# Block products with one destination share a PSUM buffer, the weight sums are spread over the products, and the tail gets a PSUM pool of its own

## The chip, the cores and the metric

The kernel runs on one core of one Trainium2 chip. The metric is the device time of one execution in microseconds. The time before is the median of three runs. Beside it there is one execution that was profiled: a record of every instruction, of every DMA and of the clock that TensorE was granted. The engines are called as in the profile: PE is TensorE's matmul, PEld its weight load, DVE is VectorE, ACT is ScalarE, POOL is GpSimd and SP is SyncE, which here only issues DMAs.

## The reference

One decoder layer on 1024 prompt rows and 8 times 8 sample rows, so 1088 rows in all, of 1024 channels. Only its end matters here: the gated FFN of width 2816, the residual and the last norm.

```
x = x + concatenate([a, o]) @ w_out
h = rms_norm(x, norm_ffn_g)
g = depthwise_conv_valid(concatenate([past, h @ w_ffn_gate]), w, b)
x = x + (silu(g) * (h @ w_ffn_up)) @ w_ffn_down      # the last FFN product
y = rms_norm(x, norm_final_g)
```

All of it is in fp32. `w_ffn_down` is 2816 x 1024.

## The kernel before

**Numbers in two parts.** An fp32 operand is split into hi (a rounded copy, made by ACT) and lo (raw minus hi, made by DVE or POOL). A product of two operands is three matmuls, hi*hi, lo*hi and hi*lo, added up in PSUM.

**The last FFN product by Strassen's scheme.** Its left operand, `w_down`, is cut into 2 x 2 blocks (a11, a12, a21, a22), and so is its right operand, the gated activations. The 22 tiles of 128 along the FFN width make two halves of 11. Of each half 5 tiles form group 0 (`STRASSEN[0]`), 4 tiles group 1, and the last 2 (`PLAIN`) are multiplied plainly in the tail. The scheme is Winograd's form: seven block products for each group in place of eight. The seven right operands, sums of activation blocks among them, were stored to DRAM in `ub` by an earlier stage (UB11, UT1, UB21, UB22, UT3, UT2, UT4). The left operands are a12, a22, a11 as they are, and then four sums of weight blocks, which `weight_sums` makes on DVE, in place.

**One block product** is done for four row tiles m of 128 output channels. For each m, `stationary` makes hi (ACT, L1362) and lo (POOL, L1363) of 128 x n*128 weights (n is 5 or 4), in a ring `AS` of 4 tiles. Then `pair()` takes a PSUM buffer of two banks, and `block_product` issues n tiles x 3 matmuls x 2 halves of 272 columns into it (L911, L913, L914): 30 matmuls in group 0, 24 in group 1. Then DVE adds the buffer to each destination (L1439), a quarter of `x2`: `x2[4*r+m]` is the residual of row block r, h is its left or right half of 544 columns. The destinations are the third member of `PRODUCTS`: 1, 1, 4, 2, 2, 3 and 1 of them. So each of the fourteen products has its own buffers, and every destination is one DVE add from PSUM: 14 adds a group and m, 112 in all.

**Order.** The program runs the products in the order a12, a22, a11, a21, a22, a11, a12. `weight_sums(g, m)`, four DVE operations (L1368 to L1371), stands in the third product, right after the block product of each m. All loads go through `load` (L1325) on SP's queue, each told to issue after the one before. Their order is that of the program: a12, moving operand 0, the left halves of `x2[0..3]`, a22, moving operand 1, two stores of the stage before, the left halves of `x2[4..7]`, a11, moving operand 2, a21, moving operand 3, the right halves of `x2`, and so on. `load_moving` brings n tiles of 128 x 544 into one of three rings of 5 (X1, X0, XA by turns), so the tiles of product q + 3 wait until product q has been multiplied. ACT makes their hi (L1347) and DVE their lo (L1348). Group 1's a12 and a22 are loaded during the fourth and fifth product of group 0, its a11 and a21 at its own first product.

**PSUM.** The pool of this stage has 3 buffers of two banks and 2 single banks (`r`) for the norm. Outside what the code says by `issue_after`, a planner orders the instructions of each engine by a model of their times.

**The tail** (`last_product`) multiplies the last 2 + 2 tiles in four column chunks (`TAIL`: 320, 256, 256, 256). For each chunk and each of eight row tiles it issues 12 matmuls (L1458 to L1460), adds the result to `x2` (L1470) and sums squares (L1472, L1476). Row tiles 2i and 2i + 1 share one buffer of two banks (`tail_bank`). During the next chunk the norm of the one before is finished (`root`, `spread`, L205, L232) and its rows are scaled (L1487) and stored (L1489).

## Time and profile before

| what | us |
|---|---|
| time, median of 3 runs | 1374.52 (1371.86 to 1377.04) |
| the profiled execution's own time | 1372.98 |
| its span, first to last instruction | 1371.2 |
| PE busy in the span | 1319.3 (96%) |
| DVE busy in the span | 965.4 (70%) |
| ACT, POOL busy in the span | 557.7 (41%), 479.0 (35%) |
| stage of the block products, first matmul to last add | 1096.3 to 1303.3 and the add that starts there |
| tail | from there to 1371.2 |

The page cuts the span into 40 slices of 34 us; the two stages above are slices 32 to 39. A busy PE says only that matmuls were in its pipe, so the number of matmuls in a stretch and the granted clock say more than the share. `x504` is a count of instructions. An answer with windows gives for each stretch the busy time and count of each engine, the granted clock, the mean share of the 16 DMA engines and the GB/s. In a list of groups, what stands behind the bar is the busy time, the mean duration of one in ns, and the idle time of the engine just before them with what ended it.

### The profile page before, as it was taken

The page shows a single profiled execution, that of the slowest core. Times are in us where ns is not written, and L with a number is a line of the kernel's source. Part 1 is how long each engine was busy: PE and PEld are TensorE (multiplying, and loading weights), DVE is VectorE, ACT ScalarE, POOL GpSimd, SP SyncE. Part 2 cuts the span into 40 slices and gives each one's busy share as a digit, 9 for nine tenths or more (in the row PEclk, how much of TensorE's full clock was granted, in tenths as well). Part 3 has the DMA queues.
Part 4 walks back from the last instruction along what each step waited for, and adds up shares of the span by engine and source line. Part 5 has one row for each costly group of instructions (what it writes and reads, how often), then busy time and mean ns, then how long its engine had stood idle before and what let it go on. Part 6 is the DMA issues. An engine that isn't in the chain of part 4 may idle for free.

```text
span 1371.2 us, 25956 instructions
## 1 busy us (share of the span) xinstructions
PE 1319.3 (96%) x10275; PEld 1249.3 (91%) x10275; DVE 965.4 (70%) x1825; ACT 557.7 (41%) x1128; POOL 479.0 (35%) x375
## 2 busy tenths in 40 slices
PE   7999999999999999999999999999999997998996
PEld 7998988898978886888999999999999997998995
DVE  6378879456676556778986767767676579679656
ACT  6312211356575556255533333333233443343432
POOL 1221112111111001630665645656545444445600
PEclk9999999999999999999999999999999999999998
DMA  8147684945689777461033323133232492342412
GB/s 283 55 134 272 229 289 163 233 125 139 182 268 282 222 249 232 137 222 56 3 117 119 119 89 120 47 104 119 98 110 82 153 359 100 126 148 89 129 40 93
DMA packets 92762, 210.28 MB, mean 153 GB/s; under 512 B 13792, under 2 KB 42720, under 8 KB 92640
## 3 DMA queue, kind: packets, MB, share of 16 engines
q1 hardware_dynamic: 92640, 208.62, 46.8%
q8 instruction: 81, 1.33, 0.4%
q14 instruction: 41, 0.34, 0.1%
HBM read 152.55 MB, written 56.04 MB: 152 GB/s over the span
## 4 chain that ended last, share of the span: by engine, by line
PE 76%; DVE 12%; DMA 6%; issue 3%; ACT 1%; SPq 1%; POOL 1%; DVEq 0%; ACTq 0%
PE g L185 6%; PE g L183 6%; PE g L184 6%; PE py L913 4%; PE py L911 4%; PE py L914 4%; PE o L735 3%; PE g L911 3%; PE g L913 3%; PE g L914 3%; PE pz L911 3%; PE s L650 3%; PE pz L913 3%; PE pz L914 3%; PE px L911 3%
## 5 line engine op out<-in xcount | busy, mean ns | idle before, releaser
L159 POOL TENSOR_TENSOR wl<-wr,wh 128x1024 fp32r<-128x1024 f32 (+1 forms) x36 | 67.5, 1877 | 343.8 <-PE g L185 263.4
L183 PE MATMUL g<-xh,wh 128*128 128x384 f32 (+1 forms) x472 | 157.9, 335 | 1.9 <-DVE qkv L450 1.2
L911 PE MATMUL g<-ux,as 128*128 128x272 f32 x504 | 147.0, 292 | 12.5 <-DVE x L1439 7.0
L184 PE MATMUL g<-xl,wh 128*128 128x384 f32 (+1 forms) x472 | 156.7, 332 | 0.0
L185 PE MATMUL g<-xh,wl 128*128 128x384 f32 (+1 forms) x472 | 156.7, 332 | 0.0
L914 PE MATMUL g<-ux,as 128*128 128x272 f32 x504 | 146.5, 291 | 0.0
L913 PE MATMUL g<-ux,as 128*128 128x272 f32 x504 | 146.1, 290 | 0.0
L1016 POOL TENSOR_TENSOR wb<-wr,wb 128x512 fp32r<-128x512 f32 x84 | 120.8, 1448 | 57.4 <-ACT wb L1015 57.4
L1363 POOL TENSOR_TENSOR as<-ar,as 128x640 fp32r<-128x640 f32 (+1 forms) x56 | 94.6, 1696 | 108.1 <-ACT as L1362 94.2
L1015 ACT ACTIVATE wb<-wr 128x512 fp32r<-128x512 f32 x84 | 52.4, 628 | 154.4 <-DVE wr L1032 94.6
L1016 POOL TENSOR_TENSOR wa<-wr,wa 128x512 fp32r<-128x512 f32 x42 | 65.9, 1571 | 134.9 <-ACT wa L1015 115.3
L911 PEld LDWEIGHTS g<-ux,as 128*128 128x128 f32 x504 | 96.4, 191 | 14.2 <-ACT ux L1347 6.4
L691 ACT ACTIVATE y<-y,m 128x128 f32<-128x128 f32 (+1 forms) x192 | 88.4, 463 | 20.3 <-DVE m L679 20.2
L914 PEld LDWEIGHTS g<-ux,as 128*128 128x128 f32 x504 | 96.2, 191 | 0.0
L913 PEld LDWEIGHTS g<-ux,as 128*128 128x128 f32 x504 | 96.1, 191 | 0.0
L654 DVE CUSTOM_DVE_ANT_0 y<-s,pmk 128x128 f32<-128x128 f32 (+1 forms) x192 | 64.1, 379 | 44.1 <-PE s L650 34.2
L183 PEld LDWEIGHTS g<-xh,wh 128*128 128x128 f32 x472 | 89.1, 189 | 5.0 <-issue 3.1
L1238 DVE SCALAR_TENSOR_TENSOR fc<-gb,prm,fc 128x1104 f32<-128x1104 f32 x44 | 82.4, 1891 | 14.9 <-ACT fc L1236 14.4
L1439 DVE TENSOR_TENSOR x<-g,x 128x544 f32<-128x544 f32 x112 | 75.0, 715 | 23.7 <-PE g L914 23.6
L185 PEld LDWEIGHTS g<-xh,wl 128*128 128x128 f32 x472 | 89.0, 189 | 2.3 <-issue 2.1
L184 PEld LDWEIGHTS g<-xl,wh 128*128 128x128 f32 x472 | 89.3, 189 | 0.5 <-issue 0.2
L396 DVE SCALAR_TENSOR_TENSOR cacc<-gp,prm,cacc 128x1024 f32<-128x1024 f32 x60 | 84.9, 1415 | 0.0
(370 smaller groups left out, 4259.8 us busy)
## 6 DMA issues: line engine op xcount, KB each, us to landing
cr<-in_kc SPq DMA_DIRECT2D x24, 768.0 KB, 6.4
cr<-in_vc SPq DMA_DIRECT2D x24, 768.0 KB, 7.6
ux<-ub SPq DMA_DIRECT2D x63, 272.0 KB, 4.3
kk<-dk SPq DMA_DIRECT2D x48, 256.0 KB, 6.0
wr<-in_w_gate SPq DMA_DIRECT2D x22, 512.0 KB, 3.3
wr<-in_w_up SPq DMA_DIRECT2D x22, 512.0 KB, 4.3
wr<-in_w_in SPq DMA_DIRECT2D x20, 512.0 KB, 5.4
ub<-u SPq DMA_DIRECT2D x18, 544.0 KB, 4.5
```

Source lines behind the costliest of these rows:

```text
L183: nc.tensor.matmul(ps[c], whi[:, k, :], xh[:, t0:t0 + n], start=(k == 0), stop=False)
L184: nc.tensor.matmul(ps[c], whi[:, k, :], xl[:, t0:t0 + n], start=False, stop=False)
L185: nc.tensor.matmul(ps[c], wlo[:, k, :], xh[:, t0:t0 + n], start=False, stop=(k == nk - 1))
L396: eng.scalar_tensor_tensor(acc[:, :S], gp[:, j:j + S], col(w0 + j), acc[:, :S], op0=ALU.mult, op1=ALU.add)
L691: nc.scalar.activation(y, y, AF.Exp, bias=m[:, 4 * g + i:4 * g + i + 1], scale=-1.0, accum_out=den[:, g, 2 * hd + u, i:i + 1])
L911: nc.tensor.matmul(ps, whi[:, k, :], xh[:, t], start=(start and k == 0), stop=False, skip_group_check=True)
L913: nc.tensor.matmul(ps, whi[:, k, :], xl[:, t], start=False, stop=False, skip_group_check=True)
L914: nc.tensor.matmul(ps, wlo[:, k, :], xh[:, t], start=False, stop=(k == nk - 1), skip_group_check=True)
L1016: nc.gpsimd.tensor_sub(lo, x, hi.bitcast(F32))
L1238: nc.vector.scalar_tensor_tensor(c[:, :W], gb[i][:, t:t + W], col(C_FW + 3 * f + t), c[:, :W], op0=ALU.mult, op1=ALU.add)
L1363: nc.gpsimd.tensor_sub(lo, raw, hi.bitcast(F32))
L1439: nc.vector.tensor_add(x, all_of(ps), x)
```

## The change

The seven products of a group are named P1 to P7 and run in units. A unit of two products runs the first for all four m, then the second for the same four m, and the second adds onto the first's PSUM buffer (`block_product(..., i == 0)` sets no start for it). The buffer is read by DVE after each product: after the first for those destinations that need the first alone, after the second for those that need both.

* Group 0: P2 | P4 | P7 | P1, P6 | P5, P3. Group 1: P2 | P7, P4 | P1, P6 | P5, P3. The adds per m are 1 + 1 + 2 + 1 + 3 + 1 + 1 = 10 in group 0 and 1 + 1 + 1 + 1 + 3 + 1 + 1 = 9 in group 1: 76 in all.
* The weight sums are the same four operations, in three places. `first_sums` (two of them) comes with group 0's P4 (for m of 2 and 3 it may go ahead of their adds) and with group 1's P2; `second_sum` with P1; `last_sum` with P5. The sum s1 takes a22's place in group 0 and gets tiles of its own in group 1.
* Loads: a11, `x2[4..5]`'s left halves and a21 now stand ahead of the two stores and of moving operand 2; then the left halves of `x2[6..7]` and the right halves. Of group 1, a11 is loaded in the unit P1, P6 of group 0, and a21, a22, a12 in its unit P5, P3, behind the moving operands of group 1's first two products. The tail's weights are loaded in the last unit, four row tiles ahead of the activations and four behind.
* PSUM: 4 buffers of two banks for the block products. When these are done the pool is closed and another opened with 6 single banks and 2 for the norm; each row tile of the tail has a bank of its own.

The number of matmuls is the same.

```diff
--- before.py
+++ after.py
@@ -1293,54 +1293,59 @@
         zf.__exit__(None, None, None)
 
 
-        zd = zones("D")
-        zd.__enter__()
-        rbank[0] = ("D", "r", 2)
-        pairs[:] = ["D", 3]
+        side = dict(side="left", reuse_waits="tile")
+        zd, zb, zt_ = [tc.tile_pool(name=s + "D", bufs=1, **kw) for s, kw in (
+            ("sb", side), ("ps", dict(space=PSUM, **side)), ("pt", dict(space=PSUM, **side)))]
+        zone["D"], zone["Dps"] = zd.__enter__(), zb.__enter__()
+        pairs[:] = ["D", 4]
 
         def wide(s, dt=F32):
             return zt("D", "SQ", SQS, s, max(n for _, n in TAIL), dt)
 
         n0 = STRASSEN[0][1]
-        OUT = ("X1", "X0", "XA")
-        RAW = {"a12": "RA", "a22": "RB", "a11": "RC", "a21": "RC"}, {"a12": "RC", "a22": "RC", "a11": "RB", "a21": "RC"}
+        OUT = ("XA", "X0", "X1")
         RAWS = {"RA": 4, "RB": 4, "RC": 12}
+        RAW = ({"a12": "RA", "a22": "RB", "a11": "RC", "a21": "RC"},
+               {"a12": "RB", "a22": "RC", "a11": "RC", "a21": "RC", "s1": "RA"})
         wide("sq")
-        for tag in OUT:
+        for tag in OUT[::-1]:
             zt("D", tag, RING, "uh", N)
         zt("D", "AS", 4, "as", 2 * n0 * P, F32R)
         for tag in ("RC", "RB", "RA"):
             zt("D", tag, RAWS[tag], "ar", n0 * P)
 
-        PRODUCTS = ((UB21, "a12", ((0, 0),)), (UT4, "a22", ((1, 0),)), (UB11, "a11", ((0, 0), (0, 1), (1, 0), (1, 1))),
-                    (UT3, "a21", ((1, 0), (1, 1))), (UT1, "a22", ((0, 1), (1, 1))),
-                    (UT2, "a11", ((0, 1), (1, 0), (1, 1))), (UB22, "a12", ((0, 1),)))
-        jobs = [(g, i) for g in range(len(STRASSEN)) for i in range(len(PRODUCTS))]
-        ring = 0
-        raws, moving, lows = {}, {}, []
+        P1, P2, P3 = (UB11, "a11", ((0, 0),)), (UB21, "a12", ((0, 0),)), (UB22, "a12", ((0, 1),))
+        P4, P5 = (UT4, "a22", ((1, 0),)), (UT1, "s1", ((1, 1),))
+        P6, P7 = (UT2, "a11", ((0, 1), (1, 0), (1, 1))), (UT3, "a21", ((1, 1),))
+        UNITS = [(0, u) for u in ((P2,), (P4,), (P7,), (P1, P6), (P5, P3))]
+        UNITS += [(1, u) for u in ((P2,), (P7, P4), (P1, P6), (P5, P3))]
+        PRODUCTS = [(g, product) for g, unit in UNITS for product in unit]
+        raws, moving, lows, done = {}, [], [], []
         loaded_last = [None]
 
         def load(dst, src):
             with tc.issue_after(loaded_last[0]) if loaded_last[0] else nullcontext():
                 loaded_last[0] = nc.sync.dma_start(dst, src).ins
 
-        def load_raw(g, key):
+        def raw_tiles(g, key):
+            tag = RAW[g][key]
+            raws[g, key] = [zt("D", tag, RAWS[tag], "ar", n0 * P)[:, :STRASSEN[g][1] * P] for _ in range(4)]
+            return raws[g, key]
+
+        def load_raw(g, *keys):
 
             j0, n = STRASSEN[g]
-            h, i = int(key[1]) - 1, int(key[2]) - 1
-            raws[g, key] = []
-            for m in range(4):
-                t = zt("D", RAW[g][key], RAWS[RAW[g][key]], "ar", n0 * P)[:, :n * P]
-                load(t, w_down[4 * h + m][:, (i * HF + j0) * P:(i * HF + j0 + n) * P])
-                raws[g, key].append(t)
+            for key in keys:
+                h, i = int(key[1]) - 1, int(key[2]) - 1
+                for m, t in enumerate(raw_tiles(g, key)):
+                    load(t, w_down[4 * h + m][:, (i * HF + j0) * P:(i * HF + j0 + n) * P])
 
         def load_moving(q):
-            g, i = jobs[q]
+            g, (b, _, _) = PRODUCTS[q]
             j0, n = STRASSEN[g]
-            b = PRODUCTS[i][0]
-            moving[q] = []
+            moving.append([])
             for j in range(j0, j0 + n):
-                t = zt("D", OUT[::-1][q % 3], RING, "ux", N, F32R)
+                t = zt("D", OUT[q % 3], RING, "ux", N, F32R)
                 hi, lo = t[:, :HN], t[:, HN:N]
                 raw = lo.bitcast(F32)
                 load(raw, ub[j][:, b * HN:b * HN + HN])
@@ -1363,14 +1368,23 @@
             nc.gpsimd.tensor_sub(lo, raw, hi.bitcast(F32))
             return [t.rearrange("p (k c) -> p k c", c=P) for t in (hi, lo)]
 
-        def weight_sums(g, m):
-            a11, a12, a21, a22 = [raws[g, k][m] for k in ("a11", "a12", "a21", "a22")]
-            nc.vector.tensor_add(a22, a21, a22)
+        def first_sums(g, m):
+            a11, a21, a22, s1 = [raws[g, key][m] for key in ("a11", "a21", "a22", "s1")]
+            nc.vector.tensor_add(s1, a21, a22)
             nc.vector.tensor_sub(a21, a11, a21)
-            nc.vector.tensor_sub(a11, a22, a11)
+
+        def second_sum(g, m):
+            a11, s1 = raws[g, "a11"][m], raws[g, "s1"][m]
+            nc.vector.tensor_sub(a11, s1, a11)
+
+        def last_sum(g, m):
+            a11, a12 = raws[g, "a11"][m], raws[g, "a12"][m]
             nc.vector.tensor_sub(a12, a12, a11)
 
         w, act = [], []
+
+        def tiles_of(j0, n):
+            return [j for i in range(2) for j in range(j0 + i * HF, j0 + i * HF + n)]
 
         def load_last(k0, k1):
 
@@ -1381,7 +1395,7 @@
                 for i in range(step):
                     load(raw[:, i * 2 * n * P:(i + 1) * 2 * n * P].rearrange("p (i c) -> p i c", i=2),
                          w_down[m0 + i].rearrange("p (i c) -> p i c", i=2)[:, :, j0 * P:(j0 + n) * P])
-                tag = ("RA", "RC", "RC", "RB")[m0 // 2]
+                tag = ("RC", "RC", "RC", "RA")[m0 // 2]
                 for i in range(step):
                     r = raw[:, i * 2 * n * P:(i + 1) * 2 * n * P]
                     hi, lo = [zt("D", tag, RAWS[tag], s, n0 * P, F32R)[:, :2 * n * P] for s in ("wh", "wl")]
@@ -1389,8 +1403,8 @@
                     nc.gpsimd.tensor_sub(lo, r, hi.bitcast(F32))
                     w.append([t.rearrange("p (k c) -> p k c", c=P) for t in (hi, lo)])
 
-        def load_act(j, q):
-            hi, lo = [zt("D", OUT[::-1][q % 3], RING, s, N, F32R) for s in ("ah", "al")]
+        def load_act(j, tag):
+            hi, lo = [zt("D", tag, RING, s, N, F32R) for s in ("ah", "al")]
             raw = lo.bitcast(F32)
             load(raw, ud[j])
             nc.scalar.activation(hi, raw, AF.Copy)
@@ -1404,54 +1418,67 @@
             behind(l, lows[4])
         load_raw(0, "a22")
         load_moving(1)
+        load_raw(0, "a11")
+        reload((4, 5), 0)
+        load_raw(0, "a21")
         for st in stores:
             load(*st)
-        reload(range(4, KT), 0)
-        for q, (g, i) in enumerate(jobs):
-            b, key, outs = PRODUCTS[i]
-            more = g + 1 < len(STRASSEN)
-            if i == 0:
-                load_raw(g, "a11")
-            if q + 2 < len(jobs):
-                load_moving(q + 2)
-            if i == 0:
-                load_raw(g, "a21")
-            if q == 1:
-                reload(range(KT), 1)
-            if i == 3 and more:
-                load_raw(g + 1, "a12")
-            if i == 4 and more:
-                load_raw(g + 1, "a22")
-            if not more:
-                if i in (3, 4, 5, 6):
-                    load_last(2 * (i - 3), 2 * (i - 3) + 2)
-                if i in (5, 6):
-                    for j in range(2):
-                        load_act(PLAIN[0] + j + (i - 5) * HF, len(jobs) + i - 5)
-            for m in range(4):
-                a = stationary(g, key, m)
-                ps = pair()
-                block_product(ps, a, moving[q], True)
-                if i == 2:
-                    weight_sums(g, m)
-                for r, h in outs:
-                    x = x2[4 * r + m][:, h * HN:h * HN + HN]
-                    nc.vector.tensor_add(x, all_of(ps), x)
+        load_moving(2)
+        reload((6, 7), 0)
+        reload(range(4, KT), 1)
+        raws[0, "s1"] = raws[0, "a22"]
+        for k, (g, unit) in enumerate(UNITS):
+            for q in range(len(moving), min(len(done) + len(unit) + 2, len(PRODUCTS))):
+                load_moving(q)
+            if k == 1:
+                reload(range(4), 1)
+            elif k == 3:
+                load_raw(1, "a11")
+            elif k == 4:
+                load_raw(1, "a21", "a22", "a12")
+            elif k == 5:
+                raw_tiles(1, "s1")
+            elif k == 8:
+                load_last(0, 4)
+                for j in tiles_of(*PLAIN):
+                    load_act(j, OUT[2 if j < HF else 0])
+                load_last(4, KT)
+            chain = {}
+            for i, product in enumerate(unit):
+                b, key, outs = product
+                for m in range(4):
+                    a = stationary(g, key, m)
+                    if i == 0:
+                        chain[m] = pair()
+                    block_product(chain[m], a, moving[len(done) + i], i == 0)
+                    if unit == (P7,):
+                        outs = ((1, 0), (1, 1))
+                    for r, h in outs:
+                        x = x2[4 * r + m][:, h * HN:h * HN + HN]
+                        added = nc.vector.tensor_add(x, all_of(chain[m]), x).ins
+                    if g and product is P2:
+                        first_sums(g, m)
+                    elif unit[0] is P4:
+                        if m < 2:
+                            half_done = added
+                        with tc.issue_after(half_done):
+                            first_sums(g, m)
+                    elif product is P1:
+                        second_sum(g, m)
+                    elif product is P5:
+                        last_sum(g, m)
+            done.extend(unit)
+        zb.__exit__(None, None, None)
+        zone["Dps"] = zt_.__enter__()
+        gbank[0], rbank[0] = ("D", "g", 6), ("D", "r", 2)
 
         nj = len(act)
-        held = [None]
-
-        def tail_bank(m):
-            if m % 2 == 0:
-                held[0] = pair()
-            return held[0][:, m % 2 * 512:m % 2 * 512 + 512]
-
 
         def last_product(t0, n, hook):
 
             acc = None
             for m in range(KT):
-                ps = tail_bank(m)
+                ps = bank(*gbank[0])
                 whi, wlo = w[m]
                 with tc.issue_after(summed[0]) if m in (2, 4) and i else nullcontext():
                     for k, (xh, xl) in enumerate(act):
@@ -1509,6 +1536,7 @@
 
             acc = last_product(t0, n, norm_of_last)
         scaled(rstd(acc, D, wide, n)[:, :n], *TAIL[-1])
+        zt_.__exit__(None, None, None)
         zd.__exit__(None, None, None)
         zr.__exit__(None, None, None)
 
```

## The prediction, made before the change was run

> **What bounds the kernel now.** First the page: which engine, and where it isn't full.
>
> ```profile
> PE 1319.3 (96%) x10275; PEld 1249.3 (91%) x10275; DVE 965.4 (70%) x1825; ACT 557.7 (41%) x1128; POOL 479.0 (35%) x375
> PE   7999999999999999999999999999999997998996
> ```
>
> PE bounds the whole. The change touches slices 32 to 39, and of these the second and the fifth show less than a full PE (the 7 and the 8 behind the long run of 9s). Next the list of groups cut to that stage: what PE waited for, and what DVE did there.
>
> ```profile
> L911 PE MATMUL g<-ux,as 128*128 128x272 f32 x504 | 147.0, 292 | 12.5 <-DVE x L1439 7.0 <-ACT ux L1347 4.8 <-ACT as L1362 0.8
> L1439 DVE TENSOR_TENSOR x<-g,x 128x544 f32<-128x544 f32 x111 | 74.3, 715 | 21.4 <-PE g L914 21.3
> L1348 DVE TENSOR_TENSOR ux<-ux 128x544 fp32r<-128x544 f32 x61 | 58.1, 977 | 16.7 <-ACT ux L1347 16.5
> L1369 DVE TENSOR_TENSOR ar<-ar,ar 128x640 f32<-128x640 f32 (+1 forms) x8 | 10.0, 1249 | 0.1
> L1370 DVE TENSOR_TENSOR ar<-ar,ar 128x640 f32<-128x640 f32 (+1 forms) x8 | 8.2, 1021 | 0.0
> L1368 DVE TENSOR_TENSOR ar<-ar,ar 128x640 f32<-128x640 f32 (+1 forms) x8 | 8.1, 1020 | 0.0
> L1371 DVE TENSOR_TENSOR ar<-ar,ar 128x640 f32<-128x640 f32 (+1 forms) x8 | 7.0, 880 | 0.0
> L1397 DVE TENSOR_TENSOR al<-al,ah 128x1088 fp32r<-128x1088 f32 x4 | 5.8, 1448 | 0.3 <-ACT ah L1396 0.3
> ```
>
> PE stood idle 12.5 us, most of it until a DVE add freed a PSUM buffer. Where, the windows say:
>
> ```profile
> 1130.00:1140.00 10.00, 5.18 (x30) 5.00 (x30) 10.00 (x14) 2.71 (x4) 1.82 (x1) 0.83 0.40 143
> 1140.00:1150.00 10.00, 8.79 (x66) 8.22 (x66) 10.00 (x16) 3.32 (x5) 4.90 (x2) 1.00 0.12 33
> 1150.00:1160.00 10.00, 8.83 (x71) 8.63 (x70) 10.00 (x16) 4.67 (x7) 5.37 (x3) 1.00 0.61 213
> 1160.00:1170.00 10.00, 8.74 (x70) 8.55 (x70) 7.59 (x10) 2.02 (x3) 4.65 (x3) 1.00 0.22 55
> 1190.00:1200.00 10.00, 10.00 (x82) 10.00 (x81) 6.46 (x10) 2.88 (x4) 5.07 (x4) 1.00 0.25 80
> 1230.00:1240.00 10.00, 9.23 (x74) 9.05 (x73) 10.00 (x11) 3.35 (x6) 6.62 (x4) 1.00 0.32 106
> 1240.00:1250.00 10.00, 8.89 (x71) 8.70 (x71) 9.96 (x14) 3.30 (x6) 4.92 (x3) 1.00 0.02 8
> 1250.00:1260.00 10.00, 7.79 (x50) 7.60 (x50) 10.00 (x17) 4.18 (x7) 2.13 (x2) 0.83 0.50 166
> ```
>
> An undisturbed 10 us hold 82 matmuls (1190). The two groups of windows lack 52 + 16 + 11 + 12 = 91 and 8 + 11 + 32 = 51. In all of them but one DVE is full, and in 1190 it isn't. The price of one matmul comes from adds that follow an undisturbed block at once:
>
> ```profile
> 1194.19 1.99 DVE L1439 TENSOR_TENSOR x<-g,x 128x544 f32<-128x544 f32 x3 [1.71 <-PE g L914]
> 1197.94 1.35 DVE L1439 TENSOR_TENSOR x<-g,x 128x544 f32<-128x544 f32 x2 [1.77 <-PE g L914]
> 1288.34 1.99 DVE L1439 TENSOR_TENSOR x<-g,x 128x544 f32<-128x544 f32 x3 [0.63 <-PE g L914]
> 1291.33 1.36 DVE L1439 TENSOR_TENSOR x<-g,x 128x544 f32<-128x544 f32 x2 [1.00 <-PE g L914]
> ```
>
> A block takes 3.75 us in group 0 and 2.99 us in group 1: 3.75 / 30 = 0.125 us a matmul. So the stage lost (91 + 51) x 0.125 = **17.7 us**, 11.4 in group 0 and 6.4 in group 1. That is more than the 12.5 idle, because the clock fell to 0.83 of full speed after the two longest gaps and matmuls then ran slower.
>
> Why there? Both places are the third product. Its four blocks last 15.0 us in group 0, and the program gives DVE in that time 16 adds (16 x 0.715 = 11.4), 16 weight sums (33.3 us for 32, so 16.7) and 5 lo halves (4.9): 33 us. In group 1 it is 32 us in 12.0. The order on DVE shows how this reaches PE:
>
> ```profile
> 1127.89 2.19 DVE L1369 TENSOR_TENSOR ar<-ar,ar 128x640 f32<-128x640 f32 x1
> ...
> 1134.18 0.71 DVE L1439 TENSOR_TENSOR x<-g,x 128x544 f32<-128x544 f32 x1
> 1135.04 0.56 PE L911 MATMUL g<-ux,as 128*128 128x272 f32 x1 [4.82 <-ACT ux L1347]
> ```
>
> An add of the product before stands behind the sums; with 3 buffers PE has nowhere to write, and it goes on right after that add ends (1134.89). The row names ACT, whose hi half ended at about the same time.
>
> **The tail** has a small wait of its own.
>
> ```profile
> PE g L1458 <- DVE x L1470: 2.9, 4, 1.2
> ```
>
> That is the list of PE's waits (us in total, times, longest). Two of them in order of time:
>
> ```profile
> 1336.99 0.42 DVE L1470 TENSOR_TENSOR x<-g,x 128x256 f32<-128x256 f32 x1
> 1337.47 0.39 PE L1458 MATMUL g<-ah,wh 128*128 128x256 f32 x1 [0.52 <-DVE x L1470]
> 1354.54 3.01 DVE L1487 SCALAR_TENSOR_TENSOR x<-x,prm,rb 128x256 f32<-128x256 f32 x6
> 1358.28 0.38 PE L1458 MATMUL g<-ah,wh 128*128 128x256 f32 x1 [1.24 <-DVE x L1470]
> ```
>
> PE starts again 0.06 us after an add ends. Two row tiles share a buffer there, so I read this as the second waiting until the first has been added. The longest, 1.24 us, comes while DVE scales six rows.
>
> **The change part by part.** *Adds.* 112 become 76, which takes 36 x 0.715 = 26 us from DVE. DVE isn't the bound on average, so this alone is worth nothing; its place is what counts.
>
> *Sums.* The same 32 operations are spread. DVE's work by product, with the same prices, is in group 0 (15.0 us each): P4 4 adds, 8 sums, 5 lo halves, 2.9 + 8.3 + 4.9 = 16.1 us; P7 5.7 + 4.9 = 10.6; P1 2.9 + 4.2 + 4.9 = 12.0; P6 8.6 + 4.9 = 13.5; P5 2.9 + 4.2 + 3.9 = 11.0. In group 1 (12.0 us each) the highest are P2, 2.9 + 8.3 + 3.9 = 15.1, and P6, 8.6 + 3.9 = 12.5; P7, behind P2, has 2.9 + 3.9 = 6.8. The overruns are 1 and 3 us, where they were 18 and 20. Four buffers let DVE be one block (3.75 or 3.0 us) later than three did. So both stalls should go, and next late is nothing but PE itself.
>
> *Chains.* The second product of a unit waits for the add of the first, in the same buffer. Three blocks lie between (9 to 11 us), against one add of 0.7: no cost unless DVE is over 9 us late. P6's three adds (2.1 us) free a buffer that P5 wants three blocks later. Since all four buffers are held by one unit, a late add hits the very next unit; behind the waiting matmul stands all of PE's queue.
>
> *Loads, group 0.* SP's queue has the same DMAs in another order: four a11 and four a21 pass moving operand 2, the two stores and up to four pieces of `x2`. What slips is moving operand 2, behind a21, 4 x 320 KB. Before, it and a21 were issued in the rows below, with the DMA engines full (a share of 1.00 in the window behind them).
>
> ```profile
> 1110.62 2.51 SPq L1325 DMA_DIRECT2D ux<-ub  x5
> 1113.17 2.95 SPq L1325 DMA_DIRECT2D ar<-in_w_down  x4
> ```
>
> ```profile
> 1110.00:1120.00 10.00, 10.00 (x82) 10.00 (x81) 4.51 (x7) 4.84 (x8) 3.44 (x3) 1.00 1.00 352
> ```
>
> ```profile
> 1111.48 0.72 DVE L1439 TENSOR_TENSOR x<-g,x 128x544 f32<-128x544 f32 x1 [1.20 <-PE g L914]
> 1115.80 2.08 ACT L1347 ACTIVATE ux<-ux 128x544 fp32r<-128x544 f32 x3 [3.53 <-DMA ux<-ub]
> ```
>
> 1.31 MB at 352 GB/s is 3.7 us. Its hi halves began at 1115.8. The add at 1111.48 ends the first product, so the third, P7, begins at 1111.4 + 15.0 = 1126.4. 11 us of cover stand against 3.7 us: nothing. P4's sums want a21 earlier than before, and it lands earlier.
>
> *Loads, group 1.* Here cover is thin. a21, a22 and a12 are behind the moving operand that takes P5's ring, which is free when P5 ends. From there 4 x 272 + 8 x 256 KB and the first a12 of 256 KB must land: 3.47 MB, 9.9 us at 352 GB/s, and then hi and lo, 0.6 + 1.3 us, with about 1 for queue and landing. That is 13 us, and P3 lasts 15.0. I cost it at nothing; at half the rate it would be 8 us late.
>
> *Tail.* Single banks take away the wait for the partner. Of 2.9 us I take 2.4, because the last of them then meets DVE's six scalings. The bounds are 0 and 2.9 plus 1 for slow restarts. The change of pool costs between 0 and one add with its semaphores (0.8), if the first bank waits for the last buffer; I take 0, the nearest row being the change into this stage, where PE had no gap. The tail's last weights are now loaded behind P5's ring as well, but row tile 4 is wanted some 7 us into the tail; nothing.
>
> **The sum.** Of the 17.7 us I leave 2 for small waits at P7 of group 0 and P2 of group 1, where DVE overruns. 15.7 + 2.4 = 18.1. The profiled execution took 1372.98 (a span of 1371.2 and 1.8 around it): 1354.9. The median of the runs is 1.5 above it: **1356.5 us**.
>
> ```profile
> 1253.56 0.36 PE L911 MATMUL g<-ux,as 128*128 128x272 f32 x1 [2.21 <-DVE x L1439]
> ```
>
> On those 2 us: this gap of 2.21 us was followed by a clock of 0.83 in the window 1250, so another as long would cost its length and some 1.7 us (10 us at 0.83). The Trainium skill, "TensorE: Matmul & The Clock Gate", section "Why this matters for your kernels", names gaps of over about 3 us; by it such a gap would cost its length alone. The trace speaks against that figure here.
>
> **The rivals.** *A stall stays (chance 0.20).* Either the start is bound by transfers (the DMA share is 1.00 at 1110, and the sums that stood ahead of the add need a21, the last of them to be loaded), and 4.8 us with their slow clock of 1.7 remain; or group 1's a12 is 5 us late. Against it: DVE, not DMA, is full through 1160. It gives 1356.5 + 6 = 1363, from 1360 to 1367.
>
> *The change doesn't do what it says (0.11).* The stalls only move: P4 and P2 have as many sums as one product can bear, and the planner, which orders by modelled times, may again put sums ahead of adds. Then little but the tail's gain is left: 1368 to 1378.
>
> *Contention, the other side (0.06).* A sum takes very different times, and an add never does:
>
> ```profile
> 1223.26 1.77 DVE L1368 TENSOR_TENSOR ar<-ar,ar 128x512 f32<-128x512 f32 x1
> 1229.88 0.69 DVE L1368 TENSOR_TENSOR ar<-ar,ar 128x512 f32<-128x512 f32 x1
> ```
>
> ```profile
> L1439 DVE TENSOR_TENSOR x<-g,x x112: 707/715/727, 1103.6 to 1303.3; 128x544 f32<-128x544 f32 x112
> ```
>
> ```profile
> L1363 POOL TENSOR_TENSOR as<-ar,as 128x512 fp32r<-128x512 f32 (+1 forms) x52 | 88.4, 1706 | 102.4 <-ACT as L1362 88.5 <-DMA ux<-ub 13.7
> ```
>
> The long ones lie beside POOL's subtractions. If spreading put all sums and lo halves beside POOL, at 1.8 us each (their mean is now 1.0), DVE would need 76 x 0.715 + 5.8 + 93 x 1.8 = 228 us in a stage that took 207 (1096.3, PE's first matmul in it, to 1303.3 in the row above): 20 us slower, less the tail's 2.4: 1374.5 + 18 = 1392. It decides from a mean of 1.6 us. Against it: POOL works 88 us of that stage, less than half of it, and the change gives it nothing more. The Trainium skill, "SBUF — State Buffer", section "Who interferes with whom", says that a DVE instruction with two SBUF inputs and a GpSimd instruction that reads SBUF block each other for the whole instruction; the rows agree, since adds (one input from PSUM) keep 707 to 727 ns.
>
> **How the numbers follow.** The forecast, 1351 to 1361, has a chance of 0.63. With the first rival, up to 1367, that is 0.83, so the range is **1351 to 1368**. Its lower end is all of 17.7 + 3.9 gone (1352.9) and what the runs scatter. A measurement of this kernel can tell about 0.5% from no change, 6.9 us: faster is the forecast and the first rival, 0.83; the same is the second, 0.11; slower is the third, 0.06.
>
> **What would show it.** In the profile after: windows of the block products with 82 matmuls each and a clock of 1.00; DVE at 10.00 in a window around P4 of group 0 and P2 of group 1 at most; 76 adds; sums still about 1.0 us; in the tail no wait of PE for an add. The prediction is wrong if PE waits for an add or for a stationary operand at P7 of group 0 or P2 of group 1, or if the tail's end doesn't follow PE because DVE's adds there come late.

## The result, and the profile after

The changed kernel takes 1354.57 us (median of 4 runs, 1352.69 to 1361.21). The kernel before took 1375.37 in the same comparison (4 runs). The ratio is 0.9861, with a 95% interval of 0.9821 to 0.9900: faster by 1.0 to 1.8%. The profiled execution took 1352.69.

The first part of the page after (the same lines of before stand in the prediction):

```profile
span 1350.9 us, 25872 instructions
...
PE 1313.0 (97%) x10275; PEld 1247.8 (92%) x10275; DVE 945.5 (70%) x1789; ACT 558.2 (41%) x1128; POOL 474.1 (35%) x375
...
PE   7999999999999999999999999999999999999996
```

The 7 and the 8 behind the long run of 9s are gone. DVE has 36 instructions fewer (1825 to 1789), the adds. The list of groups for the stage of the block products after (busy, mean ns, idle before and its end):

```profile
L1458 DVE TENSOR_TENSOR x<-g,x 128x544 f32<-128x544 f32 x75 | 51.6, 715 | 28.4 <-PE g L914 28.4
L911 PE MATMUL g<-ux,as 128*128 128x272 f32 x504 | 145.1, 288 | 1.0 <-DVE x L1458 0.9
L1378 DVE TENSOR_TENSOR ar<-ar,ar 128x640 f32<-128x640 f32 (+1 forms) x8 | 10.5, 1312 | 0.0
L1374 DVE TENSOR_TENSOR ar<-ar,ar 128x640 f32<-128x640 f32 (+1 forms) x8 | 8.6, 1079 | 0.0
L1373 DVE TENSOR_TENSOR ar<-ar,ar 128x640 f32<-128x640 f32 (+1 forms) x8 | 7.7, 981 | 1.5 <-DMA ar<-in_w_down 1.5
L1382 DVE TENSOR_TENSOR ar<-ar,ar 128x640 f32<-128x640 f32 (+1 forms) x8 | 7.7, 960 | 0.1
```

PE's idle time there fell from 12.5 us to 1.0. The 32 sums take 34.5 us, a mean of 1.08 us.

**A measure that does without the stages ahead.** In the executions of this study the stage of the block products began anywhere from 1093.5 to 1104.2 us, which has nothing to do with the change and is half the size of its effect. So I compare two lengths. *Blocks* is the time from the first to the last start of L911, which a view of one line's instructions gives (minimum, median and maximum in ns, then first and last start). *Rest* is the span less that last start. Before and after:

```profile
L911 PE MATMUL g<-ux,as x504: 282/287/564, 1096.3 to 1302.7; 128*128 128x272 f32 x168
```

```profile
L911 PE MATMUL g<-ux,as x504: 282/288/363, 1096.5 to 1286.9; 128*128 128x272 f32 x168
```

Blocks went from 206.4 to 190.4 us, the rest from 68.5 (1371.2 - 1302.7) to 64.0. There are 1509 matmuls between those two starts, and at 0.125 us each they need 188.6. So the stage lost 17.8 us before and 1.8 after, and the change gave 16.0 us there and 4.5 in the rest.

Both lengths come from the one profiled execution of each kernel. Two pairs of kernels below, which do the same in this stage, differ in it by 0.6 and by 1.5 us. A difference of that size between two kernels is no evidence.

### The profile page after: what moved, and what is told of

Its sections match the earlier page's. It is cut to its first block, busy times and chain, and to the rows that moved or that the text cites. A ratio compares the mean times of both kernels' runs of the same rounds, so it can differ in the third digit from the quotient of the medians.

```text
span 1350.9 us, 25872 instructions
## 1 busy us (share of the span) xinstructions
PE 1313.0 (97%) x10275; PEld 1247.8 (92%) x10275; DVE 945.5 (70%) x1789; ACT 558.2 (41%) x1128; POOL 474.1 (35%) x375
## 4 chain that ended last, share of the span: by engine, by line
PE 82%; DVE 8%; DMA 6%; issue 2%; ACT 1%; SPq 1%; DVEq 0%; ACTq 0%
PE g L183 6%; PE g L185 6%; PE g L184 6%; PE py L913 4%; PE py L911 4%; PE py L914 4%; PE g L911 4%; PE g L913 4%; PE g L914 4%; PE o L735 3%; PE pz L911 3%; PE pz L913 3%; PE pz L914 3%; PE px L911 3%; PE px L914 3%; PE px L913 3%
## 5 line engine op out<-in xcount | busy, mean ns | idle before, releaser
L911 PE MATMUL g<-ux,as 128*128 128x272 f32 x504 | 145.1, 288 | 1.0 <-DVE x L1458 0.9
L914 PE MATMUL g<-ux,as 128*128 128x272 f32 x504 | 145.3, 288 | 0.0
L913 PE MATMUL g<-ux,as 128*128 128x272 f32 x504 | 144.7, 287 | 0.0
L1368 POOL TENSOR_TENSOR as<-ar,as 128x640 fp32r<-128x640 f32 (+1 forms) x56 | 91.3, 1640 | 102.7 <-ACT as L1367 89.9
L911 PEld LDWEIGHTS g<-ux,as 128*128 128x128 f32 x504 | 95.0, 189 | 1.3 <-ACT as L1367 1.1
L914 PEld LDWEIGHTS g<-ux,as 128*128 128x128 f32 x504 | 94.8, 188 | 0.0
L913 PEld LDWEIGHTS g<-ux,as 128*128 128x128 f32 x504 | 94.7, 188 | 0.0
L654 DVE CUSTOM_DVE_ANT_0 y<-s,pmk 128x128 f32<-128x128 f32 (+1 forms) x192 | 64.1, 378 | 41.7 <-PE s L650 31.7
L157 ACT ACTIVATE wh<-wr 128x1024 fp32r<-128x1024 f32 (+1 forms) x36 | 29.6, 822 | 111.6 <-PE g L185 79.5
```

The costliest lines, as they stand in the source:

```text
L911: nc.tensor.matmul(ps, whi[:, k, :], xh[:, t], start=(start and k == 0), stop=False, skip_group_check=True)
L913: nc.tensor.matmul(ps, whi[:, k, :], xl[:, t], start=False, stop=False, skip_group_check=True)
L914: nc.tensor.matmul(ps, wlo[:, k, :], xh[:, t], start=False, stop=(k == nk - 1), skip_group_check=True)
L1368: nc.gpsimd.tensor_sub(lo, raw, hi.bitcast(F32))
```

## The experiments

Four explanations were open for the 16 us, since the change does four things at once: the sums were taken apart; there is a fourth PSUM buffer; 36 adds are gone; the products and loads come in another order. The table has all numbers, by the measure above. A time is a median where there were several runs. The recorded expectations count blocks to the start of the last matmul of all, which gives 0.2 to 0.3 us more.

| kernel | blocks us | rest us | time us (runs) | ratio to before, 95% interval |
|---|---|---|---|---|
| before | 206.4 | 68.5 | 1375.37 (4) | |
| after | 190.4 | 64.0 | 1354.57 (4) | 0.9861 [0.9821, 0.9900] |
| b_tail | 205.8 | 63.8 | 1369.95 (10) | 0.9952 [0.9932, 0.9972] |
| a_sharedtail | 191.9 | 68.3 | 1361.26 (4) | 0.9891 [0.9863, 0.9918] |
| b_spread | 205.5 | 68.3 | 1376.99 (10) | 1.0019 [0.9996, 1.0041] |
| a_nochain | 195.8 | 64.1 | 1357.86 (4) | 0.9858 [0.9838, 0.9877] |
| b_tail4 | 200.3 | 63.4 | 1360.54 (4) | 0.9891 [0.9852, 0.9929] |
| b_spread_tail4 | 200.3 | 63.5 | 1359.13 (1) | |
| a_nochain3 | 201.3 | 63.7 | 1366.83 (1) | |
| a_loads | 193.0 | 63.6 | 1356.47 (1) | |
| a_lastearly | 190.2 | 63.7 | 1356.71 (1) | |
| a_nohalf | 188.7 | 63.8 | 1352.41 (1) | |
| a_forced | 188.7 | 64.3 | 1352.01 (1) | |
| a_scal | 190.2 | 64.5 | 1353.10 (4) | 0.9843 [0.9807, 0.9878] |

Names with b_ are edits of the kernel before, those with a_ of the kernel after. Times of single runs are given for completeness. The argument rests on the lengths, and where the times don't bear them out, the text says so.

### The tail alone

`b_tail` gives the kernel before only the tail's own pool; `a_sharedtail` takes it from the kernel after.

```diff
...
+        zb.__exit__(None, None, None)
+        zone["Dps"] = zt_.__enter__()
+        gbank[0], rbank[0] = ("D", "g", 6), ("D", "r", 2)
...
-                ps = tail_bank(m)
+                ps = bank(*gbank[0])
```

> The kernel before with one part of the change alone: the tail has a PSUM pool of its own with a bank for each row tile; the block products keep 3 buffers and the old order. Theory (the odd row tile waits for the add of its partner, and the end of the tail follows PE): PE's four waits for L1470's successor are gone and the time falls by 2.4 to 4.2 us (4.2 is what the traces of before and after differ by in the tail). Rival (the tail's end is set by DVE's scalings and sums, whatever PE waits): PE's waits go, the time falls by under 1 us. Matmuls missing from the block products' windows stay at about 142.

`a_sharedtail`, against the kernel after, keeps the pool but puts row tiles 2i and 2i + 1 into one buffer of two banks again:

```diff
-        gbank[0], rbank[0] = ("D", "g", 6), ("D", "r", 2)
+        rbank[0], pairs[1] = ("D", "r", 2), 3
...
-                ps = bank(*gbank[0])
+                ps = tail_bank(m)
```

> The changed kernel with that part alone undone: two row tiles of the tail share a buffer of two banks again, three such buffers, in the separate pool. Theory: 2.4 to 4.2 us slower than the changed kernel, with the four waits back. Rival: under 1 us.

The rest went from 68.5 to 63.8 in the one and from 64.0 back to 68.3 in the other: 4.7 and 4.3 us, nearly twice the 2.4 of the prediction and a little over the 4.2 expected here. PE's waits in `a_sharedtail` (us in total, times, longest) show the wait of before, which the list of `b_tail` no longer has:

```profile
PE g L1492 <- DVE x L1504: 2.9, 4, 1.2
```

Why 2.9 us of waiting were worth more, the matmuls around one of them show. From the timeline of before (start, duration; idle before in brackets):

```profile
1356.64 0.28 PE L1459 MATMUL g<-al,wh 128*128 128x256 f32 x1
1356.76 0.28 PE L1460 MATMUL g<-ah,wl 128*128 128x256 f32 x1
1358.28 0.38 PE L1458 MATMUL g<-ah,wh 128*128 128x256 f32 x1 [1.24 <-DVE x L1470]
1358.50 0.28 PE L1459 MATMUL g<-al,wh 128*128 128x256 f32 x1
...
1359.68 0.28 PE L1460 MATMUL g<-ah,wl 128*128 128x256 f32 x1
1361.54 0.58 PE L205 MATMUL r<-ones,sq 128*128 128x1 f32 x4 [1.58 <-DVE sq L1476]
```

Matmuls start 0.12 us apart but are shown for 0.28, so the last one before a wait hides 0.16 us of it; and the first one after it takes 0.22 to the next start instead of 0.12. From start to start, 1.52 + 0.22 us went by where 0.24 were due: a loss of 1.50, where the row says 1.24. Shorter gaps, of 0.2 to 0.35 us more than due, stood ahead of other matmuls of the tail and went too. All in all PE's part of the tail, from its first product matmul to its last, went from 56.6 to 51.2 us. Of these 5.4 us, 0.9 came back at the end. In the timeline of after:

```profile
1338.45 0.28 PE L1487 MATMUL g<-ah,wl 128*128 128x256 f32 x1
1340.81 0.58 PE L205 MATMUL r<-ones,sq 128*128 128x1 f32 x4 [2.08 <-DVE sq L1503]
```

The last square sum is now later behind the last matmul (2.08 against 1.58), and the span ends 12.4 us behind that matmul, where it was 11.5.

### Taking the sums apart, alone

> The kernel before with the weight sums alone spread: two with the second product, one with the third, one with the fifth; old order of products, old loads, 112 adds, 3 buffers, old tail. Theory: the third product asks 11.4 + 4.2 + 4.9 = 20.5 us of DVE in 15.0 in place of 33, so 8 to 13 of the 17.7 us go: 1362 to 1366 us. Rival (the start is bound by transfers, and the sums only showed it): the gap of 4.8 us near 1130 and its slow clock stay, at most 6 us faster, 1368 or more.

```diff
-        def weight_sums(g, m):
+        def weight_sums(g, m, i):
...
+            if i == 1:
                 nc.vector.tensor_add(a22, a21, a22)
                 nc.vector.tensor_sub(a21, a11, a21)
+            elif i == 2:
                 nc.vector.tensor_sub(a11, a22, a11)
+            else:
                 nc.vector.tensor_sub(a12, a12, a11)
...
+                if i in (1, 2, 4):
+                    weight_sums(g, m, i)
```

This was a miss: no change at all. Blocks lasted 205.5 us, and the time's ratio is 1.0019. The reason is in the first starts of the sums. Of before, first sum and last sum:

```profile
L1368 DVE TENSOR_TENSOR ar<-ar,ar x8: 679/812/1778, 1123.1 to 1229.9; 128x640 f32<-128x640 f32 x4, 128x512 f32<-128x512 f32 x4
...
L1371 DVE TENSOR_TENSOR ar<-ar,ar x8: 674/814/1731, 1137.6 to 1247.9; 128x640 f32<-128x640 f32 x4, 128x512 f32<-128x512 f32 x4
```

Of `b_spread`, the same two:

```profile
L1369 DVE TENSOR_TENSOR ar<-ar,ar x8: 677/811/2193, 1125.1 to 1231.9; 128x640 f32<-128x640 f32 x4, 128x512 f32<-128x512 f32 x4
...
L1374 DVE TENSOR_TENSOR ar<-ar,ar x8: 676/815/1531, 1138.9 to 1250.7; 128x640 f32<-128x640 f32 x4, 128x512 f32<-128x512 f32 x4
```

Counted from the first matmul of the stage (1096.3 and 1099.4), the first sum ran at 26.8 and 25.7 us, the last kind began at 41.3 and 39.5. In before the sums stood in the third product, which begins at 30.0 us, and yet they began in the second; in `b_spread` the last sum stood in the fifth, which begins at 60 us at the earliest. So the planner doesn't hold a sum to its place in the program. By these starts it begins a sum about when the inputs are there, as it does with the last sums of the kernel after (below). So the edit, which was to spread the sums, left them within 2 us of where they ran before. What sums that are truly held apart would give in the old order was not run.

### Buffers and shared adds

`a_nochain` is the kernel after with a buffer and adds of its own for each product (112 adds). It keeps four buffers, the order, the loads, the sums and the tail. (The lists of destinations in P1, P5 and P7 grow with it; they are left out below.)

```diff
...
-                    if i == 0:
-                        chain[m] = pair()
-                    block_product(chain[m], a, moving[len(done) + i], i == 0)
-                    if unit == (P7,):
-                        outs = ((1, 0), (1, 1))
+                    chain[m] = pair()
+                    block_product(chain[m], a, moving[len(done) + i], True)
```

> The changed kernel without the sharing of buffers: same order, loads, sums and 4 buffers, but every product has its own buffer and all 112 adds. Theory (what stalled PE was sums and adds crowded into one product): DVE has 16 adds, 4 sums and 5 lo halves in P1, 11.4 + 4.2 + 4.9 = 20.5 us in 15.0, an overrun of 5 us that one more buffer covers in part; 2 to 6 us slower than the changed kernel, the missing matmuls behind P1 and in P6 of both groups. Rival (the 36 adds saved are what counts): most of the 16 us of the block stage come back, 12 us or more slower.

`a_nochain3` is the same with `pairs[:] = ["D", 3]`, and `b_tail4` is `b_tail` with `pairs[:] = ["D", 4]`. `b_spread_tail4` adds the edit of `b_spread` to that.

> The kernel before with its old order, loads, 112 adds and sums, but 4 buffers of two banks for the block products, and the tail's own pool. To be compared with the same at 3 buffers (b_tail: 206.1 us from the first to the last matmul of the block products, of which 189.4 are matmuls at 0.125 and 0.125 us each). Theory A (the fourth buffer is what covers DVE's backlog): 8 us or more of the 17 go, 198 or less. Theory B (the order of the products is what counts: a product with few adds between the sums and the four-add product): under 4 us go, 202 or more. Tail 63.5 us in both.

> The same with the sums also spread in the program's text (two with the second product, one with the third, one with the fifth). With 3 buffers that text changed nothing (205.7 us against 206.7), because the planner starts a sum as soon as its inputs are there, wherever it is written. Theory A: as b_tail4, within 2 us. Rival (with 4 buffers the place in the text matters): 4 us or more below b_tail4.

> The changed kernel's order, loads and sums, with no sharing of buffers (112 adds) and only 3 buffers; with 4 it took 196.0 us for the block products. Theory A: the third buffer's loss brings most of the stall back, 202 or more. Theory B: within 3 us of the 196.0.

The rows of L911 in `b_tail`, `b_tail4`, `a_nochain3` and `a_nochain`, a fence each:

```profile
L911 PE MATMUL g<-ux,as x504: 282/287/428, 1100.5 to 1306.3; 128*128 128x272 f32 x168
```

```profile
L911 PE MATMUL g<-ux,as x504: 282/287/566, 1095.1 to 1295.4; 128*128 128x272 f32 x168
```

```profile
L911 PE MATMUL g<-ux,as x504: 282/288/567, 1100.0 to 1301.3; 128*128 128x272 f32 x168
```

```profile
L911 PE MATMUL g<-ux,as x504: 282/288/481, 1096.9 to 1292.7; 128*128 128x272 f32 x168
```

The fourth buffer and the new order are two factors, tried in all four combinations. The fourth buffer is worth 205.8 - 200.3 = 5.5 us with the old order and 201.3 - 195.8 = 5.5 with the new one. The new order, with its loads, is worth 4.5 with three buffers and 4.5 with four. Sharing (36 adds fewer) takes the last 195.8 to 190.4: 5.4 us; it was tried only with four buffers in the new order, and with one profiled execution on each side. Taking the sums apart in the old order gives nothing with four buffers either (200.3 both times). So 5.5 + 4.5 + 5.4 are 15.4 of the 16.0, and the 0.6 left is between before and `b_tail`, which do the same in this stage. That these steps add up proves nothing, for they lead from one end to the other; that the first two come out alike either way does speak for them.

The times bear out the fourth buffer: the intervals of `b_tail` and `b_tail4` lie apart. They don't decide the other two steps. The intervals of `b_tail4` and `a_nochain` overlap, and `a_nochain` has the same ratio to before as the kernel after (0.9858 and 0.9861), where 5.4 us would be 0.4% between them. The 5.4 us of the sharing, and the size of the order's 4.5, are thus shown in the traces only. Neither theory for `b_tail4` (8 us or more, under 4) came out, since 5.5 lies between; `a_nochain3` came to about 201.5 in the recorded measure, just under theory A's 202.

What the 36 adds do to DVE, the windows of `a_nochain` show (PE, PEld, DVE, ACT and POOL busy with their counts; granted clock, DMA share, GB/s):

```profile
1150.00:1160.00 10.00, 7.16 (x58) 6.94 (x56) 10.00 (x10) 3.22 (x5) 6.52 (x4) 1.00 0.31 98
1160.00:1170.00 10.00, 7.83 (x50) 7.86 (x51) 10.00 (x17) 2.60 (x4) 1.38 (x1) 0.83 0.40 149
```

DVE is full here as well, and PE stands still once, for 5.0 us, until a buffer is read. In the kernel after, the same windows:

```profile
1120.00:1130.00 10.00, 10.00 (x82) 10.00 (x81) 10.00 (x11) 5.35 (x9) 5.54 (x3) 1.00 1.04 378
1130.00:1140.00 10.00, 10.00 (x82) 10.00 (x81) 10.00 (x10) 5.00 (x9) 6.84 (x5) 1.00 0.17 60
1140.00:1150.00 10.00, 10.00 (x82) 10.00 (x82) 10.00 (x13) 5.28 (x8) 3.93 (x3) 1.00 0.45 141
1150.00:1160.00 10.00, 9.08 (x73) 8.89 (x73) 10.00 (x12) 2.81 (x5) 5.80 (x3) 1.00 0.36 121
1160.00:1170.00 10.00, 9.96 (x80) 9.77 (x79) 10.00 (x15) 3.94 (x6) 3.68 (x2) 1.00 0.35 126
```

DVE is full for 50 us on end, and still PE lacks only 9 + 2 matmuls. So a full DVE doesn't hurt by itself; what counts is how far it lags behind PE, against what the buffers allow.

### The loads at the start

`a_loads` is the kernel after with the loads of group 0 in the old order (stores and `x2` ahead of a11, a21 behind moving operand 2).

```diff
-        load_raw(0, "a11")
-        reload((4, 5), 0)
-        load_raw(0, "a21")
         for st in stores:
             load(*st)
+        reload(range(4, KT), 0)
+        load_raw(0, "a11")
         load_moving(2)
-        reload((6, 7), 0)
+        load_raw(0, "a21")
```

> The changed kernel with the start's loads in the old order: the two stores and the left halves of x2[4..7] ahead of a11, then moving operand 2, then a21. The changed kernel took 190.6 us for the block products. Theory (11 us of cover, nothing): within 2 us of it. Rival (the start is bound by transfers, and the earlier a21 is part of the gain): the sums of P4 come later, P7's first stationary operand with them, and 3 us or more are lost near 1130.

Blocks grew from 190.4 to 193.0. These 2.6 us lie between the theory (within 2) and the rival (3 or more), and not far above the 1.5 by which like kernels differ. Three rows show the way of a part of it to PE, from the timelines of ACT, POOL and PE in `a_loads`:

```profile
1125.34 0.74 ACT L1367 ACTIVATE as<-ar 128x640 fp32r<-128x640 f32 x1 [4.07 <-DVE ar L1374]
```

```profile
1126.15 9.57 POOL L1368 TENSOR_TENSOR as<-ar,as 128x640 fp32r<-128x640 f32 x4 [10.40 <-ACT as L1367]
```

```profile
1129.63 0.39 PE L914 MATMUL g<-ux,as 128*128 128x272 f32 x1 [1.07 <-POOL as L1368]
```

P7's stationary operand is itself a sum with a21. In `a_loads` the first sum ran 24.2 us into the stage (1122.3), in after 19.6 (1116.1), and with the later one PE gets its operand too late. From start to start this wait cost 1.2 us. The rest of the 2.6 came near 1157 and 1162, from a wait of 0.76 us for P6's stationary operand and one of 1.41 for an add. `a_sharedtail`, whose loads are those of after, has a wait of 1.41 for an add too, so that part need not be the work of the loads.

### The last 1.8 us

In the timeline of after, DVE and PE around its one counted wait:

```profile
1141.27 0.81 DVE L1382 TENSOR_TENSOR ar<-ar,ar 128x640 f32<-128x640 f32 x1
...
1156.81 0.71 DVE L1458 TENSOR_TENSOR x<-g,x 128x544 f32<-128x544 f32 x1
```

```profile
1157.67 0.36 PE L911 MATMUL g<-ux,as 128*128 128x272 f32 x1 [0.92 <-DVE x L1458]
```

This is the chain: P6's first block waits for the add of P1's first. P1 begins three products in, at 1096.5 + 45 = 1141.5, and its first block ends 3.75 us later, at 1145.3; its add ran at 1156.8, 11.5 us late. Ahead of it DVE did, among other things, three of group 0's four last sums (L1382), whose products come only in P5, 30 us later. Three kernels ask whether that is the cause. `a_lastearly` writes the last sum beside the second one, in P1, where it runs anyway. `a_forced` holds the second and last sums behind the adds of P1 and P5. `a_nohalf` drops the tie that keeps the first sums of group 0 behind an add of P4. In this order:

```diff
                     elif product is P1:
                         second_sum(g, m)
-                    elif product is P5:
                         last_sum(g, m)
```

```diff
                     elif product is P1:
-                        second_sum(g, m)
+                        with tc.issue_after(added):
+                            second_sum(g, m)
                     elif product is P5:
-                        last_sum(g, m)
+                        with tc.issue_after(added):
+                            last_sum(g, m)
```

```diff
-                        if m < 2:
-                            half_done = added
-                        with tc.issue_after(half_done):
-                            first_sums(g, m)
+                        first_sums(g, m)
```

> The changed kernel with its last weight sum written with P1, behind the second sum, in place of P5: the sums less spread in the text. In the changed kernel's trace the last sum of group 0 ran from 1141 on, 30 us ahead of P5, so the text doesn't hold it. Theory (the planner starts a sum when its inputs are there; the text's place is worth nothing): block products 190.6 us, within 1. Rival (the place in the text counts): 3 us or more longer.

> The changed kernel with the second sum told to issue after P1's add of the same m and the last sum after P5's: the sums really spread as the text says. In the changed kernel DVE is at 10.00 from 1120 to 1170 and PE loses 1.7 us in all. Theory: DVE's full stretch breaks up, the two gaps near 1157 and 1161 go: 189.4 to 190 us. Rival (the backlog is made of adds and lo halves, not of sums): within 0.4 us of 190.6, or longer, as P6's weights come later.

> The changed kernel without the one order it writes out for the sums: group 0's first two sums just follow their add in the text, none is told to issue after the add of m = 0 or 1. Theory: that order keeps sums from standing ahead of P4's adds; without it the planner starts them when a21 lands, an add waits behind them and a matmul for its buffer: 1 to 4 us longer than 190.6. Rival (four buffers cover that): within 1 us.

`a_lastearly` changed nothing (190.2): once more, the place in the text isn't the place on DVE. In `a_forced` the loss is gone, and the row of L1382 shows the sum moved to P5 (first start 1179.6, against 1141.3 in after):

```profile
L1382 DVE TENSOR_TENSOR ar<-ar,ar x8: 810/1048/1711, 1179.6 to 1275.2; 128x640 f32<-128x640 f32 x4, 128x512 f32<-128x512 f32 x4
```

```profile
1140.00:1150.00 10.00, 10.00 (x82) 10.00 (x82) 10.00 (x15) 4.46 (x7) 2.78 (x2) 1.00 0.43 141
1150.00:1160.00 10.00, 10.00 (x82) 10.00 (x82) 6.36 (x8) 2.46 (x4) 4.69 (x3) 1.00 0.25 74
```

Its windows, the second fence, have a DVE with free time from 1150 on, where it was full up to 1170, and 82 matmuls. `a_nohalf` was a miss in sign: the tie was thought to help, but without it the loss is gone too, although the last sum runs as early as ever (L1382 first at 1136.0). Its windows tell why:

```profile
1110.00:1120.00 10.00, 10.00 (x82) 10.00 (x81) 10.00 (x9) 3.97 (x8) 5.81 (x3) 1.00 1.04 395
...
1150.00:1160.00 10.00, 10.00 (x83) 10.00 (x82) 9.64 (x10) 3.23 (x6) 6.54 (x4) 1.00 0.17 41
1160.00:1170.00 10.00, 10.00 (x83) 10.00 (x82) 8.15 (x12) 4.48 (x8) 4.10 (x3) 1.00 0.60 205
```

DVE is full from 1110 on, where the kernel after had it 5.07 us busy (of 10) while the sums were held back. One kernel starts DVE's work sooner, the other moves 4 sums behind the crowd; either brings the lag under what a chain bears. The lag itself shows it: P1's first add ran 11.5 us behind its block in after, 6.1 in `a_nohalf` (at 1152.9) and 1.5 in `a_forced` (at 1147.4), and three blocks of 3.75 us lie between. Both lengths, 188.7, are the 188.6 that PE needs. How far that holds is open, for each is one execution. `a_sharedtail`, which differs from after only in the tail, lost 1.5 us more in this stage (191.9). Its timeline of DVE shows why:

```profile
1158.12 2.19 DVE L1378 TENSOR_TENSOR ar<-ar,ar 128x640 f32<-128x640 f32 x1
1160.23 1.34 DVE L1458 TENSOR_TENSOR x<-g,x 128x544 f32<-128x544 f32 x2
1161.50 0.71 DVE L1353 TENSOR_TENSOR ux<-ux 128x544 fp32r<-128x544 f32 x1
1162.13 2.19 DVE L1382 TENSOR_TENSOR ar<-ar,ar 128x640 f32<-128x640 f32 x1
```

Sums of 0.81 us take 2.19 when they fall beside POOL, and which of them do differs between executions, for DVE's order in this stage is the same in both kernels. What the two kernels take away is of the size of that scatter. Their single times (1352.41 and 1352.01) are below the median of after, but by less than its four runs scatter; whether one of them is the faster kernel wasn't settled.

### Scalings in the tail

`a_scal` hands four of a chunk's eight scalings, in place of two, to POOL and ACT (`others=(1, 2, 4, 5)`; POOL does the first of two factors, ACT the second), since DVE's six stand ahead of the last adds.

> The changed kernel with four of the eight scalings of a finished chunk on POOL and ACT in place of two. After the last matmul the changed kernel needs 12.4 us, 0.9 more than the kernel before, and PE's last sums wait 2.1 us for DVE. Theory (DVE's six scalings, 3.0 us, hold up the last adds): the tail falls from 63.8 us by 0.5 to 1.0. Rival (the last adds wait for matmuls anyway, or POOL's rows come later): no change or longer.

A miss. DVE's timeline in after and in `a_scal`:

```profile
1334.79 2.99 DVE L1514 SCALAR_TENSOR_TENSOR x<-x,prm,rb 128x256 f32<-128x256 f32 x6
```

```profile
1334.64 3.19 DVE L1514 SCALAR_TENSOR_TENSOR x<-x,prm,rb 128x256 f32<-128x256 f32 x4
```

Four scalings beside POOL's (which ran from 1333.94 to 1337.15) took as long as six had, and the rest is 64.5 against 64.0.

## Why the prediction was right, and where it wasn't

The forecast of 1356.5 us was 1.9 above the median after. That the stall of the block products would go, and that PE waiting for DVE's adds was the stall, was right. Why it went was mostly wrong, and the sum came out well because errors of opposite kinds met: spreading the sums in the program, which carried the gain, gave nothing, while the fourth buffer gave more than a cover, and adds and loads, taken as nothing, gave something. So the closeness of the number is in part luck. Step by step:

* *What the stage loses.* 17.7 us before, 2 left: measured 17.8 and 1.8. The bound (PE waiting for a DVE add, with the clock behind it) was read rightly. That 2 and 1.8 agree is luck, as the chains below tell.
* *"The 32 operations are spread".* This step failed as a mechanism. By the working, spreading the sums was what ended the overruns of 18 and 20 us. Written into the old kernel it left the sums within 2 us of where they ran, and gave nothing (`b_spread`, `b_spread_tail4`). The demand by product was worked out from the places in the program, while the planner had started the sums earlier in both kernels. Where the last two kinds of sum were really moved, in `a_forced`, 1.7 us were gained at most. What the runs showed in its place is a sum of three: the fourth buffer 5.5 us, the order with its loads 4.5, fewer adds 5.4 (the last two by one trace on each side). The sign named for it, DVE at 10.00 in a window around P4 and P2 at most, failed too: DVE is full from 1120 to 1170.
* *"Adds: this alone is worth nothing; its place is what counts".* Wrong by the traces, where 36 adds fewer gave 5.4 us, since DVE, though not the bound on average, is full for 50 us here; the times of four runs each don't show it. "Four buffers let DVE be one block later" was right, and undersold.
* *Chains: "no cost unless DVE is over 9 us late".* It was 11.5 us late at P1, and the chain cost most of the 1.8 us. The condition was right; the place was not, since the 2 us were expected at P7 and P2.
* *Loads, group 0: "nothing".* They cost nothing. That they also gave something, 1.2 us by the wait shown and 2.6 at most, was only half seen ("it lands earlier"). Group 1: no wait for a load in the list of groups after; as expected.
* *Tail: 2.4 us, bounds 0 and 3.9.* Mis-sized: 4.3 and 4.7, over the upper bound. The mechanism was right (no wait for an add after). Idle time was taken as the cost, where a wait from start to start costs more, and smaller waits that stood in other rows, or in none, went with it. In small the sign named against it came true: the end follows PE 0.9 us later than it did. *The change of pool*: nothing, as taken; the first bank is used 0.13 us after the last block.
* *The clock after a gap of 2.21 us.* The rule drawn from it holds only sometimes, see below. It wasn't used in the sum.
* *The rivals.* A stall that stays: no. A start bound by transfers: only as far as `a_loads` shows a loss. That the planner would put sums ahead of adds again came true as to the order, but not as to its cost. Contention: the mean of a sum is 1.08 us where 1.6 would have decided.

## What to carry to other kernels

An engine with 70% average load can be full over a stretch; there the lag of that engine behind the one it feeds, and how much of it the buffers bear, decide the time. One more buffer paid with either order here; fewer instructions and an earlier start paid in the traces of the changed kernel. Where a planner orders an engine's work, the place of an operation in the program says little: look up in the trace when it started, and move it by when its data arrive or by an explicit tie. Size a matmul wait from start to start, not by the idle time that is shown.

## What the runs showed of the hardware

**The clock behind a gap.** The maximum in a row of L911 tells whether the clock fell anywhere: some 365 ns is only a slow restart, 428 and more stand in kernels whose windows show a granted clock below 1, with matmuls starting 0.227 us apart in place of 0.125. Gaps of 4.8 to 5.0 us came with such a stretch, at or near their end, in every kernel that had one (before, `b_tail4`, `b_spread_tail4`, `a_nochain`, `a_nochain3`). For gaps of 2.2 to 2.9 us both were seen. Before had it behind 2.21 us, and `b_tail` behind 2.19 but not behind 2.87; `b_spread` had up to 2.9 us (its list of PE's waits, first fence) and nowhere a clock below 1 (its row of L911, second):

```profile
PE g L911 <- DVE x L1440: 14.6, 8, 2.9
```

```profile
L911 PE MATMUL g<-ux,as x504: 282/288/367, 1099.4 to 1304.9; 128*128 128x272 f32 x168
```

The stretch has no fixed length. In windows of 1 us the granted clock is 0.50 within it, and it lasts about 3.4 us in before and twice that in `b_tail4`, where its first 2 us lie in the gap. The window that holds it there, with the last 2.5 us of a gap of 4.8, has 42 matmuls of 82:

```profile
1140.00:1150.00 10.00, 7.45 (x42) 7.48 (x43) 10.00 (x15) 0.74 (x1) 0.87 (x2) 0.66 0.19 56
```

What decides between 2.2 and 2.9 us was not found out.

**DVE beside POOL.** Four scalings took 3.19 us beside four of POOL's, 0.80 each; six took 2.99, 0.50 each, beside two; and the eight at the end of after, with no work on POOL, took 3.26, 0.41 each. Work handed to POOL there gave DVE nothing.
